# A mixture-of-experts tail: 64-slot chunks started after the first 128-slot chunk, weight places in an explicit queue

## The chip, the core and the metric

One core of a Trainium2 chip runs the whole program in one launch. The metric is device time in microseconds (us) of that core, the median of several executions. Five engines run in parallel: PE (matmul; PEld is its weight load), DVE (vector), ACT (activations), POOL and SP (which here only issues the transfers and reads registers). A profiled execution gives the traces that are quoted below.

## The reference

Two layers of a diffusion backbone over 256 latent and 256 context tokens of width 1024. What matters here is the last stage, the feed-forward part of layer 1: each token goes to the best 2 of 8 experts.

```python
logits = (t @ router_w).astype(float32)              # t: 256 x 1024
top_val, top_idx = lax.top_k(logits, 2)
gate = sum(one_hot(top_idx, 8) * softmax(top_val)[..., None], axis=1)
for e in range(8):
    out += gate[:, e:e+1] * ((silu(t @ w_gate[e]) * (t @ w_up[e])) @ w_down[e])   # 1024 -> 3584 -> 1024
```

All weights are float32 and each is read from HBM once. An expert has 3 x 1024 x 3584 of them.

## The kernel before

An expert's weights are cut into 14 chunks of 256 hidden columns, and a chunk into three units of 128 x 2048 floats (1024 KB): two halves of gate and up (`hf` 0 and 1, four of the eight k-tiles each) and one of down. 8 x 14 x 3 = 336 units are read, one transfer each, all issued by SP in one fixed order.

Two kinds of experts. `full` (lines 1314 to 1362) is for an expert with up to 128 tokens. It splits each half unit into a high and a low part (`split`, lines 232 to 239: ACT writes `wh`, DVE writes `wl`; there are three pairs of buffers) and does three matmuls per product (`mm3`, 245 to 248): 24 of 512 columns for gate and up, 2 transposes, 12 of 512 columns for down. `small` (1379 to 1439) is for an expert with up to 64 tokens and uses the weights as they are, in float32: 16 matmuls of 256 columns (32 passes in the trace) and 4 of 512 (8 passes), two at a time on halves of the array. Expert 0 is a full one. The other seven are put in order by their token count: rank 0 is a full one, ranks 1 to 6 are small ones. So there are 28 full and 84 small chunks. The order is computed on the chip into `ordi` (line 1208), and SP reads it into registers with `values_load` (line 1452) to form the addresses of the weights.

Before the experts, the routing: `L`, the choice `selr`, the slots, then in one block (lines 1176 to 1221) the gate weights (softmax) and the ranking, both chains of small DVE operations. `prep_full` (1250) gathers the tokens of a full expert on PE, `prep_small` (1271) those of three small ones, 8 matmul groups into `es` and three calls of `slots_of`.

Where weights land: `raw_unit` (217 to 230) hands out places in turn: eight `raw` buffers (three in pool `w0`, five in `w3`), and places left over from earlier tiles that `more` lists: `old` (x of the context stream), `old2` and `old3` (parts of the parameter and constant tiles), `spares`. Units 0 to 3 of expert 0 are loaded while attention still runs (line 1092). When `A[:HEAD]` is written out (line 1448), units 4 to 10 go to seven raw buffers. Unit 11, the down part of chunk 3, is asked for later.

The order of the work is the order in which the program calls things, as priorities: a compile-time scheduler fills an engine's idle time with ready work of lower priority. The order is: the four full chunks 0 to 3 of expert 0; the reading of all seven registers; `prep_small`; then 84 steps, one small chunk each, and after every third a full chunk (lines 1456 to 1466), so that the 24 full chunks left are used up at step 71 and the last 12 steps are small alone. A chunk's down part is done with the next chunk (`down(c - 1, ...)`). The last small expert also writes the output.

Of the kernel before, what the change touches and what calls it, by code (L numbers as in the profile page):

```python
# [184 lines left out]
def build(tc, I, out):  # L185
# [26 lines left out]
            n -= w[i]  # L212

    more = []
    newest = []

    def raw_unit(src, n=2048):
        turns["unit"] += 1
        i = turns["unit"] % (len(more) + sum(w[2] for w in wps))
        if i < len(more):  # L220
            r = more[i]()
            if isinstance(r, list):
                for k, h in enumerate(r):
                    nc.sync.dma_start(h, src[:, k * 1024:k * 1024 + 1024])
                return r
        else:
            wp, bufs = ring("raw")
            r = wp.tile([128, n], F32, tag="raw", bufs=bufs, name="raw")
        newest[:] = [nc.sync.dma_start(r, src).ins]
        return r  # L230
# [944 lines left out]
    ordi = sm.tile([128, NR], I32, tag="ordi", bufs=1, name="ordi")  # L1175
    with tc.issue_after(last_mask):

        mxl = sm.tile([128, 2, 4], F32, tag="mxl", bufs=1, name="mxl")
        V.tensor_reduce(out=mxl[:, :, 0], in_=L, axis=AX.X, op=ALU.max)
        V.tensor_tensor(out=L, in0=L, in1=mxl[:, :, 0:1].to_broadcast([128, 2, 8]), op=ALU.subtract)  # L1180
        S.activation(gate, L, AF.Exp)
        V.tensor_tensor(out=gate, in0=gate, in1=selr, op=ALU.mult)
        V.tensor_reduce(out=mxl[:, :, 1], in_=gate, axis=AX.X, op=ALU.add)
        V.reciprocal(mxl[:, :, 2], mxl[:, :, 1])
        V.tensor_tensor(out=gate, in0=gate, in1=mxl[:, :, 2:3].to_broadcast([128, 2, 8]), op=ALU.mult)

        cnt = sm.tile([128, 8], F32, tag="cnt", bufs=1, name="cnt")
        pp = PS()
        for t in range(2):
            PE.matmul(pp[:, 0:8], ones.to_broadcast([128, 128]), selr[:, t], start=t == 0, stop=t == 1)  # L1190
        V.tensor_copy(cnt, pp[:, 0:8])
        r3 = [128, NR, NR]
        ca = cnt[:, None, 1:8].to_broadcast(r3)
        cb = cnt[:, 1:8, None].to_broadcast(r3)
        rg = t1("rg", tuple(r3))
        re_ = t1("rq", tuple(r3))
        V.tensor_tensor(out=rg, in0=ca, in1=cb, op=ALU.is_gt)
        V.tensor_tensor(out=re_, in0=ca, in1=cb, op=ALU.is_equal)
        V.tensor_tensor(out=re_, in0=re_, in1=lt8[:, 1:8, 1:8], op=ALU.mult)
        V.tensor_tensor(out=rg, in0=rg, in1=re_, op=ALU.add)  # L1200
        rk = sm.tile([128, NR], F32, tag="rk", bufs=1, name="rk")
        V.tensor_reduce(out=rk, in_=rg, axis=AX.X, op=ALU.add)
        pm = t1("pm", tuple(r3))
        V.tensor_tensor(out=pm, in0=rk[:, None, :].to_broadcast(r3), in1=C("iota", 0, NR)[:, :, None].to_broadcast(r3),
                        op=ALU.is_equal)
        V.tensor_tensor(out=rg, in0=pm, in1=C("iota", 1, 8)[:, None, :].to_broadcast(r3), op=ALU.mult)
        V.tensor_reduce(out=rk, in_=rg, axis=AX.X, op=ALU.add)
        V.tensor_copy(ordi, rk)

        r4 = [128, 4, NR, NR]  # L1210
        pg = t1("pg", tuple(r4))
        V.tensor_tensor(out=pg, in0=rt.rearrange("p t (a e) -> p (t a) e", a=2)[:, :, None, 1:8].to_broadcast(r4),
                        in1=pm[:, None].to_broadcast(r4), op=ALU.mult)
        V.tensor_reduce(out=slr, in_=pg, axis=AX.X, op=ALU.add)

        V.memset(cap[:, 0:1], 128.0)
        V.tensor_scalar(cap[:, 1:8], pm[:, 0], 64.0, 64.0, op0=ALU.mult, op1=ALU.add)
        V.tensor_tensor(out=cnt, in0=cnt, in1=cap, op=ALU.subtract)
        cmx = sm.tile([128, 2], F32, tag="cmx", bufs=1, name="cmx")
        V.tensor_reduce(out=cmx[:, 0:1], in_=cnt, axis=AX.X, op=ALU.max)  # L1220
        V.tensor_scalar(cnti[:, 0:1], cmx[:, 0:1], 512.0, None, op0=ALU.add)
# [92 lines left out]
    def full(st, e):  # L1314

        yd = []

        def down(c, g):
            if not yd:
                yd.extend(pq.tile([128, 512], F32, tag=f"yd{i}", name=f"yd{i}") for i in range(2))  # L1320
            pt = pq.tile([128, 512], F32, tag="tr", bufs=2, name="tr")
            for m in range(2):
                PE.transpose(pt[:, m * 128:m * 128 + 128], g[:, m * 128:m * 128 + 128], ident)
            hhl = t2("hhl", (128, 2, 256), F32R)
            hh, hl = hhl[:, 0], hhl[:, 1]
            hilo(hh, hl, pt[:, :256])
            for m, wd in enumerate(split_unit(e, c * 3 + 2)):
                for q in range(2):
                    a = slice(q * 512, q * 512 + 512)
                    h = slice(m * 128, m * 128 + 128)  # L1330
                    mm3(yd[q], hh[:, h], hl[:, h], wd[0][:, a], wd[1][:, a], c == 0 and m == 0, c == NCH - 1 and m == 1)

        prev = []

        def chunk(c):
            eh, el = st.e
            if c == 1:
                st.slots()
            ps = pq.tile([128, 512], F32, tag="gu", bufs=2, name="gu")
            for hf in range(2):  # L1340
                for k2, w in enumerate(split_unit(e, c * 3 + hf)):
                    for k in range(2):
                        kt = 4 * hf + 2 * k2 + k
                        a = slice(k * 512, k * 512 + 512)
                        mm3(ps, eh[:, kt], el[:, kt], w[0][:, a], w[1][:, a], kt == 0, kt == 7)
            g = t1("sg")
            S.activation(g, ps[:, :256], AF.Silu)
            V.tensor_tensor(out=g, in0=g, in1=ps[:, 256:], op=ALU.mult)
            if c:
                down(c - 1, prev.pop())  # L1350
            prev.append(g)
            if c == NCH - 1:
                down(c, prev.pop())
                st.y = t8("y", F32R, (128, 2, 1024))
                for q in range(2):
                    a = slice(q * 512, q * 512 + 512)
                    S.activation(st.y[:, 0, a], yd[q], AF.Copy, scale=st.g)
                    V.scalar_tensor_tensor(st.y[:, 1, a], yd[q], st.g, st.y[:, 0, a].bitcast(F32), op0=ALU.mult,
                                           op1=ALU.subtract)
                scatter_full(st)  # L1360

        return [lambda c=c: chunk(c) for c in range(NCH)]

    def add_to(d, ps):
        x = xs[0][:, d]
# [13 lines left out]
    def small(st, e, last=False):  # L1379
# [20 lines left out]
        def chunk(c):  # L1400
            ps = pq.tile([128, 512], F32, tag="gu", bufs=2, name="gu")
            for hf in range(2):
                r = raw_unit(unit_at(e, c * 3 + hf))
                rs = r if isinstance(r, list) else [r[:, 0:1024], r[:, 1024:2048]]
                for k in range(4):
# [5 lines left out]
            g = t1("sg")  # L1411
            S.activation(g[64:], ps[:64, :256], AF.Silu)  # L1412
            V.tensor_tensor(out=g[64:], in0=g[64:], in1=ps[64:, :256], op=ALU.mult)  # L1413
            if c:
                down(c - 1, prev.pop())
            prev.append(g)
            if c == NCH - 1:
# [5 lines left out]
        def scatter_small(st, y):  # L1423
            gT = st.gT.bitcast(F32)
            for d2 in range(2):
                pss = [PS(), PS()]
                for j in range(2):
                    for q in range(2):
                        d = 2 * d2 + j
# [10 lines left out]

    with tc.high_priority(1):
        st0 = prep_full(None, [gate[:, t, 0:1] for t in range(2)], gm0)
    more[:] = [old] + [lambda r=r: r for r in spares[:NPRE]] + [old2, old3]
    turns["unit"] = len(more) - 1
    turns["split"], turns["raw"] = 0, 3
    A = full(st0, 0)
    HEAD = 4
    for f in A[:HEAD]:
        f()
    more[:] = [old, lambda: spares[0], old2, old3]  # L1450
    with tc.issue_after(newest[0]):
        order = [nc.values_load(ordi[0:1, r:r + 1], engines=(mybir.EngineType.SP,), min_val=1, max_val=7)
                 for r in range(NR)]
    small_sts = prep_small([1, 2, 3])
    A = A[HEAD:]
    for i in range(6 * NCH):
        if i == 2 * NCH:
            st1 = prep_full([slr[:, 2 * t + 1, 0:1] for t in range(2)], [slr[:, 2 * t, 0:1] for t in range(2)])
            A += full(st1, order[0])
        if i == 2 * NCH + 8:  # L1460
            small_sts += prep_small([4, 5, 6])
        if i % NCH == 0:
            B = small(small_sts[i // NCH], order[i // NCH + 1], i // NCH == 5)
        B[i % NCH]()
        if i % 3 == 2 and A:
            A.pop(0)()
    over = nc.values_load(cnti[0:1, 0:1], min_val=0, max_val=1024)

    with tc.If(over > 512):
# [9 lines left out]
        with tc.For_i(0, NE, 1) as ei:  # L1479
            re = sm.tile([128, 8], F32, tag="re", bufs=2, name="re")  # L1480
            nc.sync.dma_start(re, rd[bass.ds(ei, 1)].rearrange("a p c -> p (a c)"))
            for n in range(2):
                st = prep_full([re[:, 4 * n + t:4 * n + t + 1] for t in range(2)],
                               [re[:, 4 * n + 2 + t:4 * n + 3 + t] for t in range(2)])
                for f in full(st, ei):
                    f()
        nc.sync.dma_start(out, xs[0])
    dr_close()
    pq_close()
# [22 lines left out]
```

## Time and profile before

| | us |
|---|---|
| median of 3 runs | 1692.71 (1689.86 to 1693.47) |
| profiled execution | 1693.54 |
| its span, first to last instruction | 1691.8 |
| PE matmul busy / weight load busy | 1621.5 (96%) / 1248.8 (74%) |
| DVE / ACT busy | 868.2 (51%) / 642.9 (38%) |
| moved by DMA | 525.25 MB, 310 GB/s over the span |

The busy shares are means over very different stages: read the span in slices first, and then ask in each stage what the engine that matters was waiting for. A "x16" behind a row counts instructions; a time in brackets is the idle time before them and what ended it. SPq is SP's queue: a row there is the moment at which a transfer was issued, not when it landed.

### The profile page before, as it was taken

To read this page: it belongs to the slowest core of one execution; us is meant where nothing else is said; L and a number is where in the kernel's file an instruction comes from. 1 tells how busy PE (TensorE), PEld (TensorE's weight loads), DVE (VectorE), ACT (ScalarE), POOL (GpSimd) and SP (SyncE) were. 2 spreads that over 40 slices of the span, in tenths; PEclk is the share of its full clock that TensorE was granted. 3 is DMA by queue.
4 is the path that set the end of the run, shared out by engine and by line. 5 is a ranking of instruction groups with operands and counts; after the bars stand their busy time and mean duration, and the time that the engine had idled before them with its cause. 6 is when DMAs were issued, how large, how long until landed. Compare 5 with 4: busy or idle time off the path is not lost.

```text
span 1691.8 us, 28517 instructions
## 1 busy us (share of the span) xinstructions
PE 1621.5 (96%) x11576; PEld 1248.8 (74%) x11576; DVE 868.2 (51%) x1484; ACT 642.9 (38%) x1019; POOL 29.2 (2%) x31
## 2 busy tenths in 40 slices
PE   7999999999999999989999999999999999989986
PEld 5897899999999999989876555556565555555643
DVE  4545786688776666667563243335243425233511
ACT  3534574444454444445562232323232323232300
POOL 0100000000000000000100000000000000000000
PEclk9999999999999999999999999999999999999999
DMA  9425266777754666653489999999999999999996
GB/s 375 174 100 200 100 236 222 263 289 298 269 180 167 217 226 252 239 209 129 176 320 400 418 418 419 419 418 419 418 419 419 418 419 418 419 419 419 419 418 261
DMA packets 77901, 525.25 MB, mean 310 GB/s; under 512 B 9024, under 2 KB 9152, under 8 KB 18240
## 3 DMA queue, kind: packets, MB, share of 16 engines
q1 hardware_dynamic: 77760, 523.33, 78.0%
q8 instruction: 93, 1.52, 0.4%
q14 instruction: 48, 0.39, 0.1%
HBM read 522.25 MB, written 1.05 MB: 309 GB/s over the span
## 4 chain that ended last, share of the span: by engine, by line
PE 70%; DMA 23%; DVE 3%; ACT 2%; issue 1%; SPq 0%; POOL 0%; DVEq 0%; ACTq 0%; POOLq 0%
DMA raw<-in_moe 13%; PE gu L1409 10%; PE gu L247 9%; PE gu L248 8%; PE gu L246 8%; DMA prb<-in_moe 6%; PE ys L1395 4%; PE acc L246 4%; PE acc L247 4%; PE acc L248 4%; DMA spare<-in_moe 2%; PE w L247 2%; PE w L248 2%; PE w L246 2%; DMA x<-in_moe 1%; DVE wl L238 1%
## 5 line engine op out<-in xcount | busy, mean ns | idle before, releaser
L238 DVE TENSOR_TENSOR wl<-raw,wh 128x1024 fp32r<-128x1024 f32 x368 | 446.9, 1224 | 216.8 <-ACT wh L236 212.8
L236 ACT ACTIVATE wh<-raw 128x1024 fp32r<-128x1024 f32 x368 | 385.2, 1057 | 331.7 <-PE gu L247 145.5
L248 PE MATMUL gu<-fh,wl 128*128 128x256 f32 x896 | 251.7, 281 | 0.5 <-DVE wl L238 0.5
L246 PE MATMUL gu<-fh,wh 128*128 128x256 f32 x896 | 251.7, 281 | 0.0
L247 PE MATMUL gu<-fl,wh 128*128 128x256 f32 x896 | 250.5, 280 | 0.0
L1409 PE MATMUL gu<-raw,es 128*64 128x256 f32 x1488 | 181.5, 383 | 6.4 <-DMA raw<-in_moe 6.2
L1412 ACT ACTIVATE sg<-gu 64x256 f32<-64x256 f32 x84 | 31.6, 376 | 394.1 <-PE gu L1409 388.6
L246 PEld LDWEIGHTS gu<-fh,wh 128*128 128x128 f32 x896 | 169.0, 189 | 2.7 <-issue 2.7
L247 PEld LDWEIGHTS gu<-fl,wh 128*128 128x128 f32 x896 | 168.4, 188 | 1.0 <-issue 1.0
L248 PEld LDWEIGHTS gu<-fh,wl 128*128 128x128 f32 x896 | 167.8, 187 | 0.7 <-DVE wl L238 0.7
L1413 DVE TENSOR_TENSOR sg<-sg,gu 64x256 f32<-64x256 f32 x84 | 35.6, 424 | 256.4 <-ACT sg L1412 255.9
L1409 PEld LDWEIGHTS gu<-raw,es 128*64 128x64 f32 x1488 | 105.8, 137 | 65.6 <-issue 12.8
L247 PE MATMUL acc<-hl,wh 128*128 128x256 f32 x448 | 124.4, 283 | 0.0
L246 PE MATMUL acc<-hh,wh 128*128 128x256 f32 x448 | 123.8, 282 | 0.0
L248 PE MATMUL acc<-hh,wl 128*128 128x256 f32 x448 | 120.3, 283 | 0.0
L1395 PE MATMUL ys<-raw,hs 128*64 128x512 f32 x424 | 102.3, 597 | 6.6 <-DMA raw<-in_moe 5.4
L247 PE MATMUL gu<-wl,ef 128*128 128x512 f32 x224 | 93.9, 419 | 8.6 <-DVE wl L238 8.5
L246 PE MATMUL gu<-wh,ef 128*128 128x512 f32 x224 | 92.8, 415 | 8.5 <-ACT wh L236 8.5
L248 PE MATMUL gu<-wh,ef 128*128 128x512 f32 x224 | 90.0, 402 | 0.0
L247 PEld LDWEIGHTS acc<-hl,wh 128*128 128x128 f32 x448 | 85.6, 191 | 0.0
L246 PEld LDWEIGHTS acc<-hh,wh 128*128 128x128 f32 x448 | 85.5, 191 | 0.0
L248 PEld LDWEIGHTS acc<-hh,wl 128*128 128x128 f32 x448 | 83.2, 191 | 0.0
(447 smaller groups left out, 2531.3 us busy)
## 6 DMA issues: line engine op xcount, KB each, us to landing
raw<-in_moe SPq DMA_DIRECT2D x223, 1024.0 KB, 17.4
raw<-in_ffn SPq DMA_DIRECT2D x84, 1024.0 KB, 4.9
spare<-in_moe SPq DMA_DIRECT2D x31, 1024.0 KB, 19.6
x<-in_moe SPq DMA_DIRECT2D x28, 1024.0 KB, 19.7
prb<-in_moe SPq DMA_DIRECT2D x27, 1024.0 KB, 18.8
rx<-in_ada SPq DMA_DIRECT2D x19, 1024.0 KB, 5.1
raw<-in_ada SPq DMA_DIRECT2D x18, 1024.0 KB, 4.8
cst<-in_moe SPq DMA_DIRECT2D x27, 512.0 KB, 18.6
```

The costliest lines, as they stand in the source:

```text
L236: S.activation(hi, r, AF.Copy)
L238: V.tensor_tensor(out=lo, in0=r, in1=hi.bitcast(F32), op=ALU.subtract)
L246: PE.matmul(o, wh, rh, start=start, stop=False, **kw)
L247: PE.matmul(o, wh, rl, start=False, stop=False, **kw)
L248: PE.matmul(o, wl, rh, start=False, stop=stop, **kw)
L1395: PE.matmul(yd[0][64 * q:64 * q + 64, :], h[:, m * 64:m * 64 + 64], rs[m][:, q * 512:q * 512 + 512], start=c == 0 and m == 0, stop=c == NC ...
L1409: PE.matmul(ps[64 * q:64 * q + 64, :256], st.e[:, kt], rs[k // 2][:, a:a + 256], start=kt == 0, stop=kt == 7, tile_position=(0, 64 * q))
L1412: S.activation(g[64:], ps[:64, :256], AF.Silu)
L1413: V.tensor_tensor(out=g[64:], in0=g[64:], in1=ps[64:, :256], op=ALU.mult)
```

## The change

After the preloading of expert 0's chunks 0 to 3, now with unit 11 too, only chunk 0 is computed first. Small chunks start right behind it, and the preloaded chunks 1 to 3 are put at steps 5, 11 and 17; the other 24 full chunks are spread over steps 18 to 81. The gate and up part of a full chunk stands ahead of that step's small chunk and its down part behind it. Places come from a queue `places` that starts with four (`spares[0]`, `old2`, `old3`, `old`) and gets two or three raw buffers more as each preloaded chunk has used them. A register is read when its expert's first unit is asked for. The softmax moves behind the ranking. In the last small chunk the down part of the chunk before stands between the two halves, and the last scatter takes its four PSUM banks from two tags of two.

```diff
     def raw_unit(src, n=2048):
-        turns["unit"] += 1
-        i = turns["unit"] % (len(more) + sum(w[2] for w in wps))
+        if places:
+            f = places.pop(0)
+            places.append(f)
+            i = 0 if f else len(more)
+        else:
+            ...
@@ routing: the seven lines of the softmax stand behind V.tensor_copy(ordi, rk) now
@@ full
-            if c:
-                down(c - 1, prev.pop())
             prev.append(g)
+
+        def rest(c):
+            down(c, prev.pop(0))
             if c == NCH - 1:
-                down(c, prev.pop())
                 st.y = t8("y", F32R, (128, 2, 1024))
@@ small
             for hf in range(2):
+                if hf and last and c == NCH - 1:
+                    down(c - 1, prev.pop())
                 r = raw_unit(unit_at(e, c * 3 + hf))
...
-            if c:
+            if prev:
                 down(c - 1, prev.pop())
@@ scatter_small
-                pss = [PS(), PS()]
+                pss = [PS(), PS()] if not last else [
+                    pq.tile([128, 512], F32, tag=t, bufs=2, name="b") for t in ("gu", "tr")]
@@ main order
-    A = full(st0, 0)
-    HEAD = 4
-    for f in A[:HEAD]:
-        f()
-    more[:] = [old, lambda: spares[0], old2, old3]
-    with tc.issue_after(newest[0]):
-        order = [nc.values_load(ordi[0:1, r:r + 1], ...) for r in range(NR)]
+    more[:] = [lambda: spares[0], old2, old3, old]
+    places[:] = [None]
+    for u in range(4, 3 * HEAD):
+        first[u] = raw_unit(unit_at(0, u))
+    places[:] = more
+    def by_rank(r):
+        if r not in order:
+            order[r] = nc.values_load(ordi[0:1, r:r + 1], ...)
+        return order[r]
+    with tc.issue_after(newest[0]):
+        by_rank(1)
+    A = full(st0, 0)
+    A[0][0]()
     small_sts = prep_small([1, 2, 3])
-    A = A[HEAD:]
+    A[0][1]()
+    due = {6 * k - 1: k for k in range(1, HEAD)}
+    i0 = 6 * (HEAD - 1)
+    for k in range(HEAD, 2 * NCH):
+        due[i0 + (k - HEAD) * (6 * NCH - i0) // (2 * NCH - HEAD)] = k
     for i in range(6 * NCH):
...
+        k = due.get(i)
+        if k is not None:
+            A[k][0]()
         B[i % NCH]()
-        if i % 3 == 2 and A:
-            A.pop(0)()
+        if k is not None:
+            A[k][1]()
+            if k < HEAD:
+                places += [None] * (2 if k == 1 else 3)
```

## Rows read from the trace of the kernel before

**Rows 1.** The page: the span in 40 slices of 42.3 us.
```profile
DMA  9425266777754666653489999999999999999996
GB/s 375 174 100 200 100 236 222 263 289 298 269 180 167 217 226 252 239 209 129 176 320 400 418 418 419 419 418 419 418 419 419 418 419 418 419 419 419 419 418 261
```

**Rows 2.** Windows: length, busy PE, PEld, DVE, ACT, POOL, clock, DMA share, GB/s.
```profile
843.58:930.00 86.42, 86.42 (x486) 59.76 (x486) 45.63 (x57) 42.59 (x61) 0.00 (x0) 1.00 0.91 353
846.00:858.00 12.00, 12.00 (x58) 10.06 (x58) 10.08 (x12) 10.30 (x15) 0.00 (x0) 1.00 1.00 396
930.00:1660.00 730.00, 695.01 (x4254) 408.53 (x4250) 261.03 (x414) 196.07 (x285) 0.00 (x0) 0.99 1.01 419
```

**Rows 3.** Timeline of SP: when transfers of expert weights were issued (start, length).
```profile
823.12 1.42 SPq L229 DMA_DIRECT2D raw<-in_moe  x2
843.58 0.36 SPq L229 DMA_DIRECT2D spare<-in_moe  x1
...
845.92 0.33 SPq L229 DMA_DIRECT2D raw<-in_moe  x1
```

**Rows 4.** Lines 1208, 1452: count, ns min/median/max, first and last start.
```profile
L1208 DVE CAST ordi<-rk x1: 161/161/161, 838.9 to 838.9; 128x7 int32<-128x7 f32 x1
L1452 SPq TENSOR_LOAD <-ordi x7: 262/263/472, 839.1 to 842.8; - x7
```

**Rows 5.** Landing times of tile `spare` (815 to 1000) and of `raw` (800 to 845).
```profile
DMA to landing us min/median/max: 4.7/10.1/18.9
...
DMA to landing us min/median/max: 4.8/6.6/9.6
```

**Rows 6.** Timeline of the head, and its group for line 1280 (busy, mean ns).
```profile
842.26 0.48 PE L246 MATMUL gu<-wh,ef 128*128 128x512 f32 x1
847.86 1.28 ACT L1347 ACT_TABLE_LOAD   x1
854.91 1.23 DVE L238 TENSOR_TENSOR wl<-x,wh 128x1024 fp32r<-128x1024 f32 x1 [0.44 <-ACT wh L236]
L1280 PE MATMUL b<-gms,ht 128*128 128x192 f32 x32 | 6.7, 326 | 0.0
862.55 0.51 PE L1241 MATMUL b<-slr,gms 128*128 128x1 f32 x4
```

**Rows 7.** The chain that ended last, 905 to 925: start, length, what.
```profile
909.50 0.23 PE yd L246
...
912.05 0.26 PE tr L1388 x2
912.32 3.38 PE gu L1409 x29
...
917.69 0.27 PE tr L1388 x2
```

**Rows 8.** Timeline after the last full chunk: PE, until it waits for a transfer again.
```profile
1599.90 0.73 PE L1374 MATMUL b<-gT,y 128*128 128x256 f32 x4
1623.79 1.95 PE L1409 MATMUL gu<-raw,es 128*64 128x256 f32 x16 [0.55 <-DMA raw<-in_moe]
```

**Rows 9.** Timeline of the end.
```profile
1672.43 1.95 PE L1409 MATMUL gu<-raw,es 128*64 128x256 f32 x16 [0.45 <-DMA raw<-in_moe]
1674.42 0.38 ACT L1412 ACTIVATE sg<-gu 64x256 f32<-64x256 f32 x1 [7.09 <-PE gu L1409]
1674.83 0.42 DVE L1413 TENSOR_TENSOR sg<-sg,gu 64x256 f32<-64x256 f32 x1 [4.76 <-ACT sg L1412]
1675.02 1.94 PE L1395 MATMUL ys<-x,hs 128*64 128x512 f32 x8 [0.64 <-DMA x<-in_moe]
1677.26 0.29 DVE L1390 COPY hs<-tr 128x128 f32<-128x128 f32 x1 [2.00 <-PE tr L1388]
1677.60 1.94 PE L1395 MATMUL ys<-spare,hs 128*64 128x512 f32 x8 [0.38 <-DVE hs L1390]
1683.20 1.13 PE L1430 MATMUL b<-gT,ys 64*128 64x256 f32 x4 [0.89 <-DVE x L1366]
```

More of the change, by code (lines that the diff above doesn't have):

```diff
@@ L214, in build @@
     more = []
+    places = []
     newest = []
     def raw_unit(src, n=2048):
-        turns["unit"] += 1
-        i = turns["unit"] % (len(more) + sum(w[2] for w in wps))
+        if places:
[3 more added lines that the diff above has]
+        else:
+            turns["unit"] += 1
+            i = turns["unit"] % (len(more) + sum(w[2] for w in wps))
+            f = more[i] if i < len(more) else None
         if i < len(more):
-            r = more[i]()
+            r = f()
             if isinstance(r, list):
                 for k, h in enumerate(r):
-                    nc.sync.dma_start(h, src[:, k * 1024:k * 1024 + 1024])
+                    newest[:] = [nc.sync.dma_start(h, src[:, k * 1024:k * 1024 + 1024]).ins]
                 return r
@@ L1176, in build @@
     with tc.issue_after(last_mask):
[L1178 to L1185, printed above, removed]
         cnt = sm.tile([128, 8], F32, tag="cnt", bufs=1, name="cnt")
@@ L1208, in build @@
         V.tensor_copy(ordi, rk)
+        mxl = sm.tile([128, 2, 4], F32, tag="mxl", bufs=1, name="mxl")
+        V.tensor_reduce(out=mxl[:, :, 0], in_=L, axis=AX.X, op=ALU.max)
+        V.tensor_tensor(out=L, in0=L, in1=mxl[:, :, 0:1].to_broadcast([128, 2, 8]), op=ALU.subtract)
+        S.activation(gate, L, AF.Exp)
+        V.tensor_tensor(out=gate, in0=gate, in1=selr, op=ALU.mult)
+        V.tensor_reduce(out=mxl[:, :, 1], in_=gate, axis=AX.X, op=ALU.add)
+        V.reciprocal(mxl[:, :, 2], mxl[:, :, 1])
+        V.tensor_tensor(out=gate, in0=gate, in1=mxl[:, :, 2:3].to_broadcast([128, 2, 8]), op=ALU.mult)
         r4 = [128, 4, NR, NR]
@@ L1360, in chunk @@
                 scatter_full(st)
-        return [lambda c=c: chunk(c) for c in range(NCH)]
+        return [(lambda c=c: chunk(c), lambda c=c: rest(c)) for c in range(NCH)]
     def add_to(d, ps):
@@ L1442, in build @@
         st0 = prep_full(None, [gate[:, t, 0:1] for t in range(2)], gm0)
-    more[:] = [old] + [lambda r=r: r for r in spares[:NPRE]] + [old2, old3]
-    turns["unit"] = len(more) - 1
+    HEAD = 4
     turns["split"], turns["raw"] = 0, 3
-    A = full(st0, 0)
-    HEAD = 4
-    for f in A[:HEAD]:
-        f()
-    more[:] = [old, lambda: spares[0], old2, old3]
-    with tc.issue_after(newest[0]):
-        order = [nc.values_load(ordi[0:1, r:r + 1], engines=(mybir.EngineType.SP,), min_val=1, max_val=7)
-                 for r in range(NR)]
-    small_sts = prep_small([1, 2, 3])
-    A = A[HEAD:]
+    more[:] = [lambda: spares[0], old2, old3, old]
[3 more added lines that the diff above has]
+    places[:] = more
+    order = {}
+    def by_rank(r):
+        if r not in order:
+            order[r] = nc.values_load(ordi[0:1, r:r + 1], engines=(mybir.EngineType.SP,), min_val=1, max_val=7)
+        return order[r]
+    with tc.issue_after(newest[0]):
+        by_rank(1)
+    A = full(st0, 0)
+    A[0][0]()
+    small_sts = prep_small([1, 2, 3])
+    A[0][1]()
[3 more added lines that the diff above has]
+        due[i0 + (k - HEAD) * (6 * NCH - i0) // (2 * NCH - HEAD)] = k
     for i in range(6 * NCH):
@@ L1458, in build @@
             st1 = prep_full([slr[:, 2 * t + 1, 0:1] for t in range(2)], [slr[:, 2 * t, 0:1] for t in range(2)])
-            A += full(st1, order[0])
+            A += full(st1, by_rank(0))
         if i == 2 * NCH + 8:
@@ L1462, in build @@
         if i % NCH == 0:
-            B = small(small_sts[i // NCH], order[i // NCH + 1], i // NCH == 5)
+            B = small(small_sts[i // NCH], by_rank(i // NCH + 1), i // NCH == 5)
+        k = due.get(i)
+        if k is not None:
+            A[k][0]()
         B[i % NCH]()
-        if i % 3 == 2 and A:
-            A.pop(0)()
+        if k is not None:
+            A[k][1]()
+            if k < HEAD:
+                places += [None] * (2 if k == 1 else 3)
+    places[:] = []
+    turns["unit"] = 0
     over = nc.values_load(cnti[0:1, 0:1], min_val=0, max_val=1024)
@@ L1484, in build @@
                                [re[:, 4 * n + 2 + t:4 * n + 3 + t] for t in range(2)])
-                for f in full(st, ei):
-                    f()
+                for k, f in enumerate(steps := full(st, ei)):
+                    f[0]()
+                    if k:
+                        steps[k - 1][1]()
+                steps[-1][1]()
         nc.sync.dma_start(out, xs[0])
```

## The prediction

> **What bounds the kernel now.** I read the page's slices first [rows 1]. From slice 23 on the DMA engines are busy in nine tenths or more and move 418 or 419 GB/s, whatever PE does; in slices 19 to 21 they move 129, 176 and 320 GB/s. So the last half of the span is set by the reading of weights, and the stretch before it wastes reading time. The windows say the same [rows 2]: 930 to 1660 runs at 419 GB/s and a DMA share of 1.01, 843.58 (the first transfer of a routed expert) to 930 at 353. A unit of 1.049 MB therefore takes 2.50 us of reading, and a small or full chunk 7.5 us. SP's timeline [rows 3] shows where the stretch begins: expert 0's seven raw units are issued by 824.5, then nothing for 19 us. The two lines of the order [rows 4] tell why: `ordi` is written from 838.92 to 839.08, seven register reads begin at 839.1, and the first routed transfer is issued at 843.58. Last I read the end [rows 9] for what follows the last landing, and the dense stretches of PE [rows 7] for what a chunk costs it: a small one 5.64 us (transposes at 912.05 to transposes at 917.69), a full one 36 x 0.23 + 0.3 for its transposes, with switches some 8.9 us.
>
> Everything up to 824 is untouched. The end moves by what the stream of transfers gains or loses, plus what comes after its last landing. I work against the profiled execution's own 1693.54 us (span 1691.8); the median of the runs, 1692.71, lies 0.8 lower, and I put the sum on the median.
>
> **The change part by part.**
>
> *Register read when needed, ranking before softmax.* Seven reads and their address arithmetic took 839.1 to 843.5, 0.63 us each [rows 3, 4]. One is left ahead of the first transfer: 6 x 0.63 = 3.8 us earlier. The two DVE chains alternate now; the ranking first should save the two delays of 0.2 us or so that it suffers, 0.4 us. The softmax finishes that much later, behind the gathering for expert 0, which keeps PE until 842. First routed transfer at 839.4: **-4.2 us** (bounds -3.7 to -4.5). The six other reads are met later in SP's queue; there SP issues one transfer in 2.5 us of reading and waits for a place in between, so 0.6 us each costs nothing, and 0.6 each where that cover is missing.
>
> *Unit 11 preloaded.* The eighth raw buffer was first used at 845.92 [rows 3], though no expert weight is read from about 830 to 843. It is now filled with unit 11 behind the seventh, in idle reading time, so one unit less has to be read afterwards: **-2.5 us** (bounds -2.5 to 0, should the buffer come free late).
>
> *What the reading loses after its first routed transfer.* Before: (419 - 353)/419 x 86.4 = 13.6 us up to 930 [rows 2], partly its start, mostly waiting for raw buffers that four full chunks hold. After: the start costs 4.7 us to the first landing [rows 5] less 2.5 of reading, 2.2. Only four places exist at first, and the fourth, `old`, holds the down weights of chunk 0, so four units are in by about 854 and then the reading stops until PE has done half a small chunk. PE starts at 842.26 and must first do chunk 0's gate and up (to 847.9, where ACT loads silu's table), `prep_small` (32 instructions, 8 x 0.65 = 5.2; three `slots_of` at some 0.6 = 1.9), and chunk 0's down part, 0.3 + 12 x 0.23 = 3.1 [rows 6, 7]: 858.1. The first half unit takes 1.7 more (half of 3.38). If the scheduler fills gaps as it did before, where pieces of `prep_small` stood between matmuls, I take 858.3 for the fifth transfer's issue (bounds 854.5 and 861). It lands at 863.0, where unbroken reading would have had it at 844.1 + 4 x 2.5 = 854.1: 8.9 lost.
>
> From there four places must sustain the rate. A place's round is 4.7 to land, 1.95 of matmuls, about 0.4 to release and issue: 7.1 us, against the 10.0 us that four units take to read. It holds with 2.9 us to spare. A shallow queue read 396 GB/s in 846 to 858 [rows 2], 5.5% under the deep one: over some 26 us, 1.5 us. Chunk 1's gate and up at step 5 keep PE for 5.6 us, 2.7 more than the spare time, if they stand in one piece; filled into PE's gaps of 7.5 - 5.64 = 1.9 us per small chunk they cost nothing; I take 1.0. After that six, nine and twelve places carry any full chunk. Sum 2.2 + 8.9 + 1.5 + 1.0 = 13.6 us, the same as before: **0 us** (bounds -7 and +8). What was a wait for raw buffers becomes a wait for the first small chunk.
>
> *Spreading the full chunks.* 2.75 small chunks per full one ask 2.75 x 5.64 + 8.9 = 24.4 us of PE in 28.1 us of reading, so the reading still sets the pace: **0**. It ends with the last full chunk at step 81 instead of 71. When it and its scatter were done before, at 1600.6, PE was behind: it ran 22.6 us without a wait, to 1623.2, through 12 units that take 30.0 us to read [rows 8]. It was 7.4 us late, 2.8 of it because two down parts stood together, now one: 4.6. A small unit gives back (7.5 - 5.64)/3 = 0.62 us. After step 81 six units are left, three of which may be done ahead of the scatter: 0.9 to 2.7 us late at the end. **+1.8 us** (bounds 0 and +5).
>
> *The last chunk.* Before, the last but one landing released the down part (1675.02) and the last one came in time for 1677.60 [rows 9]. Now the second half lands last but one, at about 1675.0 on that scale, and 1.95 + 0.38 + 0.42 + transposes 0.27 + copy 0.29 with their gaps, 3.6 us, follow before the last down part: 1678.5 against 1677.6, **+0.9** (bounds 0 and +1.6). Two more PSUM tags remove the 0.89 us that the last scatter matmuls waited; the eight additions, at 0.41 one after the other, then end 0.4 us earlier: **-0.4** (bounds -0.9 and 0).
>
> **Sum:** -4.2 - 2.5 + 0 + 0 + 1.8 + 0.9 - 0.4 = -4.4 us. 1692.7 - 4.4 = **1688.3 us**.
>
> The Trainium skill speaks against the four places: in DMA: Bandwidth & Descriptors, section Bandwidth, 1 MB moved by itself reaches 341 GB/s, 16 MB 425. The row with a shallow queue shows 396 here, so the trace agrees in direction. By the page's figure 26 us of reading would lose 4.8 us and not 1.5, and the estimate would be 1691.6.
>
> **The rivals.**
>
> *1. Gain and new loss cancel.* The first small chunk starts only at 861 (+2.7), chunk 1 stands in one piece (+1.7): 1692.7. For it: every routed transfer past the fourth waits for PE, and PE has no gap from 842 to 858. Against it: `prep_small` was mixed finely with other work. The case that PE, not the reading, sets the pace belongs here: PE is busy 695 of 730 us in 930 to 1660 [rows 2], and no PE work is removed, so the time would stay within a microsecond. The rate of 419 GB/s without a dip, and weight loads busy only 409 of these 730, speak against it.
>
> *2. Four places starve the reading (slower).* If a place's round in the first six steps is not 7.1 but over 10 us, each microsecond costs 18/4 = 4.5 us over their 18 units. The preloads took up to 9.6 us to land [rows 5]; 9.6 + 1.95 + 0.4 = 12.0 gives +9.0, and the time is 1697.3. It turns the forecast to a loss from a round of about 11 us. Against it: a 9.6 us landing needs other transfers in front, which four places hardly allow.
>
> *3. The head overlaps better.* Small matmuls fill PE's gaps from 848 on, the fifth transfer goes out at 854.5 and chunk 1 costs nothing: -3.8 - 1.0, with no lag at the end -1.8: 1681.7. For it: the scheduler did put other work between full matmuls [rows 6]. Against it: nothing shows PE idle in this stretch.
>
> **How the numbers follow.** The measurement tells about 0.2%, 3.4 us, from no change. Forecast 0.42 (nearly all of it faster: 0.38), rival 1 0.33, rival 2 0.13, rival 3 0.12. Faster 0.38 + 0.12 = 0.50; same 0.04 + 0.33 = 0.37; slower 0.13. The range reaches from rival 3 to the middle of the way to rival 2, 1682.0 to 1694.5; the forecast case alone is 1685 to 1691.
>
> **What would show it.** In the changed trace: SP issues the first routed transfer near 839.4, with one register read ahead; an eighth raw unit is issued before 830; the fifth routed transfer near 858.3; the mean rate from the first routed transfer to 930 again near 353 GB/s. After 930 it stays at 419. Near the end PE does not wait for the last units, or waits less than before. I am wrong on the sum if the reading is even from 845 on (rival 3), if rates under 380 GB/s go on past step 6 (rival 2), or if the time from the last landing to the end grows by over 5 us.

## The result and the profile after

The changed kernel takes 1714.18 us (median of 4 runs, 1711.92 to 1715.52) against 1693.09 for the kernel before beside it: ratio 1.0121, 95% interval 1.0102 to 1.014. It is slower by 21 us; I had forecast 1688.3 and a range up to 1694.5. The profiled execution took 1714.5, its span is 1712.7, so the two spans differ by 20.9 us.

The page's slices of the changed kernel, against [rows 1]:

```profile
DMA  9425366777644666652689599999999999999995
GB/s 377 165 99 197 121 223 219 287 290 285 262 176 164 218 250 245 240 212 108 246 329 400 227 416 419 418 419 418 419 418 419 419 419 419 418 419 419 419 419 228
```

Slices 19 to 22 (108, 246, 329, 400) are much as before. New is a hole where 418 had stood: slice 23 (942 to 985) moves 227 GB/s. The windows place it (columns as in [rows 2]):

```profile
838.54:930.00 91.46, 82.91 (x530) 50.96 (x529) 25.78 (x48) 25.46 (x45) 0.00 (x0) 0.98 0.86 332
930.00:980.00 50.00, 37.91 (x226) 20.51 (x224) 11.61 (x18) 8.89 (x13) 0.00 (x0) 0.92 0.64 255
980.00:1680.00 700.00, 676.22 (x3988) 383.76 (x3989) 264.70 (x401) 203.04 (x292) 0.00 (x0) 1.00 1.01 419
```

From 930 to 980 the reading loses (419 - 255)/419 x 50 = 19.6 us; after that it is as even as before. SP's timeline shows both ends of the head and of the hole (start, length; it answers to [rows 3]):

```profile
799.90 22.38 SPq L236 DMA_DIRECT2D raw<-in_moe  x8
838.54 0.36 SPq L236 DMA_DIRECT2D spare<-in_moe  x1
...
848.79 0.34 SPq L236 DMA_DIRECT2D x<-in_moe  x1
855.92 0.33 SPq L236 DMA_DIRECT2D spare<-in_moe  x1
...
867.76 0.33 SPq L236 DMA_DIRECT2D spare<-in_moe  x1
...
930.16 0.33 SPq L236 DMA_DIRECT2D spare<-in_moe  x1
930.70 25.59 SPq L236 DMA_DIRECT2D raw<-in_moe  x2
956.56 0.33 SPq L236 DMA_DIRECT2D prb<-in_moe  x1
957.14 0.33 SPq L231 DMA_DIRECT2D cst<-in_moe  x1
```

Two transfers into `raw` stand in one row of 25.59 us: the first goes out at 930.70, the second at 955.96, and everything behind it in SP's fixed order (`prb`, `cst`, `x`, `spare`) waits with it. SP's waits from 905 to 965 (total, times, longest) name the one that held it:

```profile
SPq L236 <- DVE wl L245: 24.7, 1, 24.7
```

And the timeline before and around its end:

```profile
915.61 2.96 PE L1418 MATMUL gu<-raw,es 128*64 128x256 f32 x16
...
940.41 1.23 DVE L245 TENSOR_TENSOR wl<-raw,wh 128x1024 fp32r<-128x1024 f32 x1 [6.99 <-ACT wh L243]
...
945.61 1.22 DVE L245 TENSOR_TENSOR wl<-raw,wh 128x1024 fp32r<-128x1024 f32 x1 [0.73 <-ACT wh L243]
...
951.86 0.50 PE L253 MATMUL yd<-wh,hhl 128*128 128x512 f32 x1
...
954.51 0.39 PE L255 MATMUL yd<-wh,hhl 128*128 128x512 f32 x1
954.71 2.54 DVE L245 TENSOR_TENSOR wl<-raw,wh 128x1024 fp32r<-128x1024 f32 x2 [1.90 <-ACT wh L243]
...
955.96 0.33 SPq L236 DMA_DIRECT2D raw<-in_moe  x1
...
960.76 1.98 PE L1402 MATMUL ys<-raw,hs 128*64 128x512 f32 x4 [5.60 <-DMA raw<-in_moe]
```

The transfer waits for a split (`wl`) that empties its buffer: it goes out at 955.96, and the first of the two splits in the row of 954.71 ends at 955.93. Counted through from chunk 0, this is the second half of unit 9. Unit 9 belongs to chunk 3 of expert 0, the third preloaded one, whose turn is step 17; its split needs a `wh` and a `wl` buffer that chunk 2's down part (`yd`, to 954.9) has just given back. So the buffer that SP wanted from 931 on was not one that a finished chunk had freed: it was one still full.

In the code an entry `None` of `places` says only "a raw buffer"; which pool it comes from is told by `ring("raw")`, whose eight turns, counted from unit 4 on, are five of pool `w3` and then three of `w0`. Units 4 to 8 had taken the five turns of `w3`, units 9 to 11 the three of `w0`. The queue's first five raw transfers (906.18, 906.72, 916.45, 918.61, 930.70) fell to `w3` again and had to wait there for 1.6 us at most. They did not go into five different buffers: the last splits of units 7 and 8, counted in the same way, are the rows of 940.41 and 945.61, and the transfer of 918.61 waited for the matmuls in the row of 915.61, a small chunk that read what the transfer of 906.18 had brought. SP's waits from 916.9 to 919:

```profile
SPq L236 <- PE gu L1418: 1.6, 1, 1.6
```

The sixth raw transfer is the turn of `w0`. All three buffers there held units of chunk 3, and it had to wait for the first of them, while in `w3` the buffer of the transfer of 916.45, read until 932.5, lay free. PE ran dry at 955.2 and stood for 5.60 us (the last row of the timeline), until that transfer had landed.

At the end (against [rows 9]):

```profile
1692.58 1.89 PE L1402 MATMUL ys<-raw,hs 128*64 128x512 f32 x8
1694.30 1.90 PE L1418 MATMUL gu<-raw,es 128*64 128x256 f32 x16
1697.13 0.33 PE L1395 MATMUL tr<-cst,sg 64*128 64x64 f32 x2 [0.94 <-DVE sg L1422]
1697.85 1.94 PE L1402 MATMUL ys<-raw,hs 128*64 128x512 f32 x8 [0.38 <-DVE hs L1397]
1700.57 2.00 PE L1440 MATMUL b<-gT,ys 64*128 64x256 f32 x16 [0.79 <-ACT ys L1429]
1701.74 3.22 DVE L1373 SCALAR_TENSOR_TENSOR x<-b,ada,x 128x256 f32<-128x256 f32 x8 [3.95 <-PE b L1440]
```

The last unit lands at 1693.75 by the landing records (1677.35 before): 16.4 of the 20.9 us. PE doesn't wait for it, nor for the one before, as it did in [rows 9]: it is late. From the last landing to the end of the last addition it is 1704.96 - 1693.75 = 11.2 us, before 7.9. The remaining 1.2 us lie behind that addition, where 5.6 to 7.8 us passed in all these kernels with the same work: a difference between executions that nothing here explains.

### The profile page after: what moved, and what is told of

Its sections match the earlier page's. It is cut to its first block, busy times and chain, and to the rows that moved or that the text cites. A ratio compares the mean times of both kernels' runs of the same rounds, so it can differ in the third digit from the quotient of the medians.

```text
span 1712.7 us, 28498 instructions
## 1 busy us (share of the span) xinstructions
PE 1635.3 (95%) x11576; PEld 1235.7 (72%) x11576; DVE 865.8 (51%) x1484; ACT 641.0 (37%) x1019; POOL 29.2 (2%) x31
## 5 line engine op out<-in xcount | busy, mean ns | idle before, releaser
L245 DVE TENSOR_TENSOR wl<-raw,wh 128x1024 fp32r<-128x1024 f32 x332 | 402.3, 1223 | 214.8 <-ACT wh L243 213.1
L243 ACT ACTIVATE wh<-raw 128x1024 fp32r<-128x1024 f32 x332 | 346.9, 1057 | 323.3 <-PE gu L254 146.5
L1418 PE MATMUL gu<-raw,es 128*64 128x256 f32 x1424 | 175.5, 386 | 0.9 <-DMA raw<-in_moe 0.9
L1418 PEld LDWEIGHTS gu<-raw,es 128*64 128x64 f32 x1424 | 96.5, 137 | 69.2 <-issue 26.1
L1402 PE MATMUL ys<-raw,hs 128*64 128x512 f32 x440 | 109.3, 620 | 12.3 <-DMA raw<-in_moe 11.2
```

What stands on the lines that cost most here:

```text
L243: S.activation(hi, r, AF.Copy)
L245: V.tensor_tensor(out=lo, in0=r, in1=hi.bitcast(F32), op=ALU.subtract)
L1402: PE.matmul(yd[0][64 * q:64 * q + 64, :], h[:, m * 64:m * 64 + 64], rs[m][:, q * 512:q * 512 + 512], start=c == 0 and m == 0, stop=c == NC ...
L1418: PE.matmul(ps[64 * q:64 * q + 64, :256], st.e[:, kt], rs[k // 2][:, a:a + 256], start=kt == 0, stop=kt == 7, tile_position=(0, 64 * q))
```

## The experiments

Medians with the ratio to the kernel before in the same session (1692.1 us for experiments 1 to 4, 1694.35 for 5 to 8, 1693.45 for 9 to 12). "1, ..." in the second column means the kernel of experiment 1 with that further edit.

| | kernel | us | ratio (95%) |
|---|---|---|---|
| 1 | freed raw buffers named as places | 1704.35 | 1.0076 (1.0063 to 1.0089) |
| 2 | ring kept, raw places only after chunk 3 (four runs: two at 1699 to 1700, two at 1709) | 1704.37 | 1.0068 (1.0043 to 1.0092) |
| 3 | 1, last full chunk at step 71 | 1696.43 | 1.0032 (1.002 to 1.0044) |
| 4 | before, with late registers and ranking first | 1691.61 | 1.0004 (0.9989 to 1.0019) |
| 5 | 1, second full expert lighter | 1700.39 | 1.0039 (1.0021 to 1.0058) |
| 6 | 3, three chunks preloaded | 1686.59 | 0.9966 (0.9951 to 0.998) |
| 7 | 3, old end | 1695.11 | one run |
| 8 | 4, unit 11 preloaded | 1693.13 | 0.9995 (0.9983 to 1.0008) |
| 9 | 1, full chunk behind the small one | 1693.63 | 1.001 (1.0001 to 1.002) |
| 10 | 1, expert 0 lighter | 1695.29 | 1.0015 (1.0004 to 1.0027) |
| 11 | 6, old end | 1686.65 | 0.9964 (0.9952 to 0.9976) |
| 12 | 6, spread to step 81 | 1696.43 | 1.002 (1.0007 to 1.0033) |

### Is it the ring's turn? (1 and 2)

Experiment 1 changes nothing but which raw buffer a new place is:

```diff
-                places += [None] * (2 if k == 1 else 3)
+                places += [lambda r=first[u]: r for u in range(max(4, 3 * k), 3 * k + 3)]
```

> The queue's raw places name the very buffers that a preloaded chunk has just freed, instead of taking the next of the ring of eight. Theory (the ring): the changed kernel stood from 930.7 to 956.3 because the ring's turn had come to the buffer of unit 9, which chunk 3 still held, though the buffers of units 4 and 5 had long been used up and free. Then SP's wait of 24.7 us on wl is gone, the 19.6 us of reading lost between 940 and 980 come back, and the time is 1694 to 1696 us. Rival (too few places: any six places would have been empty while PE does chunk 2 at step 11): at most a third comes back, 1707 us or more. What is lost at 850 to 870 and 890 to 920 (about 15 us) stays under both.

Experiment 2 keeps the ring and adds its eight buffers only when chunk 3 is done:

```diff
-            if k < HEAD:
-                places += [None] * (2 if k == 1 else 3)
+            if k == HEAD - 1:
+                places += [None] * 8
```

> The ring is kept, but all eight raw places are added at once after chunk 3 (step 17), when none is held any more; steps 0 to 17 run on four places. Theory (the ring): no wait of SP over 10 us in the head; each of chunks 1 to 3 costs at most 5 us of reading, so 1695 to 1705 us, faster than the changed kernel with fewer places for longer. Rival (too few places): four places for twelve more steps lose more, 1716 us or above.

The windows of experiment 1:

```profile
930.00:980.00 50.00, 47.03 (x305) 25.98 (x302) 14.06 (x24) 9.69 (x15) 0.00 (x0) 1.00 1.01 418
1200.00:1250.00 50.00, 43.33 (x238) 25.27 (x237) 15.50 (x21) 12.69 (x17) 0.00 (x0) 0.93 1.01 419
1250.00:1310.00 60.00, 55.72 (x339) 32.71 (x337) 27.21 (x45) 17.79 (x25) 0.00 (x0) 1.00 0.87 344
```

The hole is gone, 418 where 255 stood, and so is the wait of 24.7 us; experiment 2 has no long wait for `wl` either (6.2 us in all from 830 to 1060). (It loses 12.0 us more evenly, 377 GB/s from 930 to 1050, since its places come late.) That the ring's turn made the first hole is shown. But the time fell by only 10 us, not by 19.6: a second hole opened, (419 - 344)/419 x 60 = 10.7 us from 1250 to 1310, where the changed kernel ran at 419. Experiment 2, set back by its 12.0 us, runs at 419 there too.

### What is the second hole? (5, 9, 10)

Counting landed and consumed units in the trace, PE falls from 1 unit behind the reading at 1100 to 10 behind at 1300; with the part that is in work all twelve places are then held, and SP waits for PE and for splits. In the changed kernel the first hole had set the reading back, and by the same count PE was under six units behind there. PE is idle for 6.7 of the 50 us before the hole, though units lie ready. Its timeline there:

```profile
1203.09 1.90 PE L1418 MATMUL gu<-raw,es 128*64 128x256 f32 x16
1205.92 0.33 PE L1395 MATMUL tr<-cst,sg 64*128 64x64 f32 x2 [0.94 <-DVE sg L1422]
1206.54 0.50 PE L253 MATMUL gu<-wh,ef 128*128 128x512 f32 x1 [0.29 <-ACT wh L243]
1207.80 0.55 PE L254 MATMUL gu<-wl,ef 128*128 128x512 f32 x1 [0.76 <-DVE wl L245]
1208.15 0.63 PE L255 MATMUL gu<-wh,ef 128*128 128x512 f32 x1
...
1212.02 0.39 PE L253 MATMUL gu<-wh,ef 128*128 128x512 f32 x1
```

At this passage from a small to a full chunk PE meets a row of waits, since its order is fixed at compile time: transposes that need the small chunk's `sg`, then `wh`, then `wl`. Waits of 0.94, 0.29 and 0.77 come back one full chunk later, from 1239.73 on. Experiment 5 made the wrong chunks lighter:

```diff
-                        mm3(ps, eh[:, kt], el[:, kt], w[0][:, a], w[1][:, a], kt == 0, kt == 7)
+                        (mm3 if isinstance(e, int) else mm2)(ps, eh[:, kt], el[:, kt], w[0][:, a], w[1][:, a],
+                                                             kt == 0, kt == 7)
```

(the down product likewise; `mm2` is `mm3` without its second matmul of `wh`.)

> The kernel with each freed raw buffer named as a place (the first experiment), in which the second full expert (rank 0, 14 chunks) is left without the product of the high part of the weights and the low part of the tokens: two matmuls per product instead of three, 12 fewer per chunk, 12 x 0.23 = 2.8 us less of PE work in each of its chunks and some 39 us over the expert. That part of the computation is left out. Theory (the reading loss of about 10.7 us between 1250 and 1310 comes from PE, which consumes a unit in about 2.9 us there while the reading delivers one in 2.50, until all twelve places are held): the rates of 1250 to 1310 stay above 400 GB/s, no wait of SP for PE over 5 us in 1200 to 1400, and the time falls by about 10 us against the first experiment, to 1692 to 1697. Rival (the places or the order of the queue still hold the reading up there, whatever PE has to do): the rates of 1250 to 1310 fall to 250 to 390 again and the time stays within 3 us of 1704.

The dip stayed (344 from 1250 to 1310), and this says nothing on PE: expert 0's fourteen chunks run up to 1300, so the lightened expert begins behind the stretch. (What it gained is behind the dip: from the last landing to the end of the last addition 9.3 us, in experiment 1 11.1.) Experiment 10 puts the same edit where it bears (`mm2 if isinstance(e, int) and c > 3`):

> As the experiment that lightened the second full expert, but for expert 0, whose chunks are the ones that run up to 1300: its chunks 4 to 13 are left without the product of the high part of the weights and the low part of the tokens, 12 matmuls x 0.23 = 2.8 us less of PE work in each; that part of the computation is left out. Seven of these chunks fall into 1100 to 1300: 19 us less work where PE fell 9 units of 2.5 us behind the reading. Theory (PE's pace there fills all twelve places and stops the reading): PE's arrears stay under six units, the rates of 1250 to 1310 stay above 400 GB/s and the time is 1693 to 1697. Rival (something else than PE's pace holds the places): the loss of 10 us stays, 1702 to 1706.

```profile
1200.00:1250.00 50.00, 40.23 (x246) 20.65 (x242) 15.40 (x23) 13.30 (x19) 0.00 (x0) 1.00 1.01 419
1250.00:1310.00 60.00, 56.24 (x345) 33.03 (x345) 29.46 (x49) 19.05 (x27) 0.00 (x0) 1.00 1.01 418
```

No dip, and 1695.29: PE's pace holds the places there. (By the count above PE was at most 3.4 units behind from 1100 to 1310, inside what I expected.) Experiment 9 leaves all work in and moves a full chunk behind its step's small one, as before:

```diff
-        if k is not None:
+        if k is not None and k < HEAD:
             A[k][0]()
         B[i % NCH]()
+        if k is not None and k >= HEAD:
+            A[k][0]()
         if k is not None:
             A[k][1]()
```

> The kernel with each freed raw buffer named as a place (the first experiment, 1704.3), with both parts of a full chunk behind the small chunk of its step, as before; the three preloaded chunks stay as they are. In the first experiment PE is idle for 6.7 of the 50 us from 1200 to 1250, in waits for the splits of a full chunk that stand behind the activation of the small one, though 7 to 10 units lie there unused. Theory (the order around a full chunk makes these waits): PE busy over 47 of 50 us in 1200 to 1250, no rate under 400 GB/s in 1250 to 1310, about 1694. Rival (the waits come from when the units land, or from the amount of work, and not from this order): the loss of some 10 us stays and the time is 1702 to 1706.

```profile
1200.00:1250.00 50.00, 48.28 (x294) 28.92 (x295) 20.40 (x30) 16.09 (x22) 0.00 (x0) 1.00 1.02 419
1250.00:1310.00 60.00, 58.26 (x356) 34.55 (x354) 27.58 (x45) 18.15 (x25) 0.00 (x0) 1.00 1.01 416
```

The whole work is the same, and in 1200 to 1250 PE is busy for 48.28 us instead of 43.33, there is no dip, and the time is 10.7 us less than in experiment 1. Absolute windows catch the two executions at slightly different work (the first routed transfer went out at 842.27 in experiment 1 and at 835.51 here), so I take a longer one as well, experiment 1 first:

```profile
1100.00:1300.00 200.00, 185.65 (x1102) 110.66 (x1100) 75.30 (x128) 57.19 (x89) 0.00 (x0) 0.98 0.99 405
```

```profile
1100.00:1300.00 200.00, 195.09 (x1176) 117.54 (x1175) 84.22 (x138) 64.96 (x97) 0.00 (x0) 1.00 1.01 418
```

PE is idle for 14.4 us in one and 4.9 in the other. So with the same work the order around a full chunk decides whether the second hole opens. It is not the only way to close it: less work closes it too (experiment 10). The edit also puts the full chunk's transfers behind the small one's in SP's queue; which of the two orders matters was not separated.

The Trainium skill (Perfetto Trace Analysis, section Optimization Strategy) says that the same gap repeating on the engine that should be saturated can mean too few buffers for the next tile. Here most of the gaps went with the same buffers in another order (PE's waits in 1200 to 1250 fall from 6.6 us to 1.7), so in this case the measurement decides against that reading.

### The spread, the head and the end (3, 6, 12, 7, 11)

Experiment 3 ends the full chunks at step 71, as before:

```diff
-        due[i0 + (k - HEAD) * (6 * NCH - i0) // (2 * NCH - HEAD)] = k
+        due[i0 + (k - HEAD) * (5 * NCH + 4 - i0) // (2 * NCH - HEAD)] = k
```

> As e1_own, and the last full chunk stands at step 71 instead of 81 (the spacing is 2.33 small chunks). Theory of the tail: PE is late at the end because only six units follow the last full chunk; with 36 it catches up, and the time from the last landing to the end falls from about 18.6 us to about 15, so 3 to 4 us less than e1_own. Rival: the last landing itself moves later by as much because full chunks stand denser, and the time is that of e1_own within 1 us.

It gains 7.9 us: from the last landing to the end of the last addition 11.1 us become 8.3 (2.8), and the second hole shrinks (385 GB/s from 1250 to 1310, 4.9 us instead of 10.7). Experiment 6 then preloads three chunks, so that three raw buffers are places from the start:

```diff
-    HEAD = 4
+    HEAD = 3
-    places[:] = more
+    held = []
+    for _ in range(3):
+        wp, bufs = ring("raw")
+        held.append(wp.tile([128, 2048], F32, tag="raw", bufs=bufs, name="raw"))
+    places[:] = more[:3] + [lambda r=r: r for r in held] + more[3:]
```

> The kernel with own places and with the last full chunk at step 71 (the third experiment, 1696.4), with three of expert 0's chunks preloaded instead of four, so that three raw buffers are places from the start: seven places, not four. Theory (four places starve the reading in the head): SP's idle time between the fourth and the eighth routed transfer, some 11 us, shrinks to about 3, and the dips of 890 to 910 go, 11 us in all, but three units or 7.5 us more are left to read: about 1692 to 1693. Rival (the head is held by PE, which has chunk 0, the gathering and the first chunks to do whatever the places are, so the gain only moves the wait to the next place that PE must free): the three units cost their 7.5 us and the time is 1700 to 1704.

```profile
836.66:930.00 93.34, 92.16 (x610) 58.08 (x609) 29.43 (x52) 29.02 (x51) 0.00 (x0) 1.00 0.95 385
...
1200.00:1250.00 50.00, 49.81 (x301) 29.31 (x301) 23.57 (x39) 18.54 (x29) 0.00 (x0) 1.00 1.01 417
1250.00:1310.00 60.00, 57.95 (x342) 33.62 (x342) 23.64 (x36) 16.25 (x22) 0.00 (x0) 1.00 1.01 419
```

1686.59: faster than both kernels, against before by 0.34% (0.2 to 0.49). From its first routed transfer (836.66) to 930 the reading loses (419 - 385)/419 x 93.34 = 7.6 us; in the changed kernel, from 838.54 on, 19.0. That is 11.4 won for 7.5 paid, much as expected. I had expected 1692.5 in all; the rest is the second hole, 4.9 us in experiment 3, which isn't there. Experiment 12 asks why not, by spreading its full chunks to step 81 again:

> The kernel with three preloaded chunks, with the other 25 full chunks spread over steps 12 to 81 instead of 12 to 71, as in the change. Theory (three preloaded chunks remove the head's loss and keep PE under the limit of the places; the late full chunks cost only at the end): no rate under 400 GB/s between 930 and 1660, from the last landing to the end 3 to 4 us more than 14.0, the time about 1690. Rival (the shorter spread is what keeps PE on pace in 1200 to 1310): the dip comes back, 1698 or more.

```profile
1250.00:1310.00 60.00, 58.42 (x350) 33.15 (x350) 23.13 (x43) 14.60 (x23) 0.00 (x0) 0.97 0.99 388
```

The dip is back, as the rival had it (its time of 1698 is not reached), and with the longer end (11.3 us from the last landing to the end of the last addition, 8.3 in experiment 6) it costs 10 us. The amount of work done doesn't explain it: by 1100 experiment 6 has done 9.7 full chunks and is 1.8 units behind, this one 8.4 and 4.8. Which property of the spread makes the scheduler's order leave fewer waits is open.

Experiments 7 and 11 put the down part of the last chunk but one back behind both halves:

```diff
-                if hf and last and c == NCH - 1:
-                    down(c - 1, prev.pop())
```

> The kernel with own places and the last full chunk at step 71, with the down part of the last chunk but one behind the last gate and up again, as before. Theory (the down part between the halves costs what I predicted, 0.9 us, since the second half is then late): from the last landing to the end 13.0 us instead of 13.9. Rival (the end hangs on work behind the last matmul alone): 13.9, no difference over 0.3.

> The kernel with three preloaded chunks (1686.6), with the down part of the last chunk but one behind the last gate and up again. From the earlier look at that edit, which shortened the stretch from the last landing to the end from 13.9 to 12.85: 1.0 us less, about 1685.6. Rival (that look showed a scatter of one execution): 1686.6, no difference.

From the last landing to the end of the last addition: 8.28 us to 7.25 in the first pair, 8.28 to 7.35 in the second. (The first pair has one run of the kernel with the old end.) The stretch is shorter by what the prediction put on it; in the time of the whole, 1686.65 against 1686.59, a microsecond is not seen.

### The two gains alone (4 and 8)

Both on the kernel before, with its order and its turn of places: 4 reads a register when it is needed and puts the ranking first (of its edit only the reading is shown here), 8 also preloads unit 11.

```diff
-        order = [nc.values_load(ordi[0:1, r:r + 1], ...) for r in range(NR)]
+        by_rank(1)
```

> The kernel before with two edits of the change alone: a register is read when its expert is due, and the softmax stands behind the ranking. Theory of the prediction's first term: the first routed transfer goes out 4 us earlier and the end moves by 4 us, to 1689 us. Rival: after four early units the reading waits for raw buffers that the full chunks free on PE's time (before: issues at 853.0, 859.6, 863.3), so the 4 us are given back within 15 us and the time stays within 1 us of before.

```diff
+    for u in range(4, 3 * HEAD):
+        first[u] = raw_unit(unit_at(0, u))
+    turns["unit"] = 12
     A = full(st0, 0)
```

> The kernel before with registers read when needed, the ranking ahead of the softmax, and unit 11 preloaded into the eighth raw buffer; order, turn of the buffers and all else as before. Theory of the prediction (a unit read ahead of the routing is one unit less to read afterwards): 2.5 us less than with late registers alone, about 1689. Rival (the reading of 840 to 930 is bound by the places that PE has to free, so an earlier unit only waits in its buffer and holds that place longer): within 1 us of 1691.6.

The same window of both, 4 first:

```profile
843.58:930.00 86.42, 86.42 (x487) 58.91 (x486) 44.11 (x54) 39.86 (x57) 0.00 (x0) 1.00 0.88 342
```

```profile
843.58:930.00 86.42, 86.42 (x487) 58.61 (x487) 43.82 (x54) 39.69 (x57) 0.00 (x0) 1.00 0.84 331
```

The first routed transfer goes out at 836.88 and 836.58, 6.7 and 7.0 us earlier than before (3.3 and 3.6 of it because all work up to there ran earlier in these executions: the first preload at 798.27 and 797.96, before at 801.55), and unit 11 is there. But the mean rate falls from 353 [rows 2] to 342 and 331, and PE is busy for all of the 86.42 us in each. The last unit lands 2.4 and 2.5 us earlier than before, less than that shift alone, and neither time differs from before by 0.2%. Units that come earlier wait earlier for PE to free a place.

## Why the prediction was wrong

What it had right: the start (first routed transfer at 838.54, forecast 839.4; the first register read came at 837.5, 1.6 us earlier than in [rows 4], since the work ahead ran earlier), the eighth raw unit ahead of 830, one register read ahead (the six others were not met later in the queue, as I had thought: they came from 841.6 to 844.4, while SP had to wait for the fifth place anyway), the fifth routed transfer at 855.92 (forecast 858.3, bounds 854.5 to 861), 419 GB/s from 980 to 1680.

The step that failed is the sentence "After that six, nine and twelve places carry any full chunk", which closed the term of what the reading loses. I counted places and did not ask which buffer each entry was. I had described the raw buffers as added when a chunk has used them; the code only adds turns. The diff that I quoted has `None` entries, and `raw_unit` sends them to the ring; laid beside the preloaded units, the sixth turn falls on the pool whose three buffers hold units 9 to 11. With buffers of its own the same queue runs at 418 GB/s from 930 to 980 (experiment 1). This is 19.6 us, outside the bounds of -7 and +8 on that term. None of the three rivals had it.

The same term was 5.4 us too low before 930 as well: 19.0 lost from 838.54 on, not 13.6. The place `spare` came round at 855.92, 867.76, 879.30 and 893.09, in 11.5 to 13.8 us, over the 10.0 that four units take to read. I had put 7.1, with 4.7 for the landing and no wait for PE. The landings of `spare` from 855 to 900:

```profile
DMA to landing us min/median/max: 4.9/6.7/9.4
```

In the three rounds the landing took 4.9, 9.4 and 7.9 us, and in the first and the third the unit then lay for 5.0 and 3.9 us until PE, busy with other work, read it. This is the second rival, whose 9.6 us for a landing I had argued away. Experiment 6, with three places more, loses 7.6 us there and not 19.0.

The term of the spread, "so the reading still sets the pace: 0", looks right in the changed kernel only because its reading had been set back. Without the ring's fault it costs 10.7 us. I had divided PE's work (24.4 us) by the reading time (28.1) and left out two things: the waits inside PE's fixed order, 14.4 us from 1100 to 1300 in experiment 1, and the gathering and scattering of tokens where experts change, some 24 us of busy PE in the same 200 us (gathering 11.4, scattering 8.6, slots 3.7). The time that my division leaves free there, 200 x (28.1 - 24.4)/28.1 = 26 us, does not hold both.

The two gains, -4.2 and -2.5, are real as events and worth nothing as time in the order of before (experiments 4 and 8). My first rival named this (gain and loss cancel, with PE as the pace), at 0.33. What they are worth in the changed order was not run.

The end was about right: +0.9 + 1.8 - 0.4 = +2.3 forecast, 11.2 - 7.9 = 3.3 measured. By parts: the down part between the halves 1.0 and 0.9 (experiments 7 and 11; forecast 0.9), PE's lateness 2.8 (experiment 3; forecast 1.8), the PSUM tags, from the start of the last scatter to the end of the additions, 4.92 to 4.39, -0.5 (forecast -0.4).

The sum against the profiled executions: -5.0 (start) - 2.5 (unit 11) + 5.4 (head) + 19.6 (hole) + 3.3 (end) + 1.2 (behind the last addition) = 22.0, measured 20.9. Of the 1.1 left over, 1.0 lies in the last 17.35 us before the last landing, where the reading lost 4.3 us before (316 GB/s) and loses 3.3 now (340).

So the mended change (own buffers, three preloaded chunks, the last full chunk at step 71 as before) is worth 0.34%. Mended in the buffers alone it is still 12 us slower than the kernel before (experiment 1). Three chunks together with full chunks behind the small ones were not run.

## What to carry to other kernels

When one engine issues all transfers in a fixed order, write out for each issue which buffer it goes into and what must have read it; a count of free places proves nothing, and one place taken too early stops all that are free behind it. A transfer that starts earlier is only worth something if the place after it also comes free earlier. And a hole upstream hides those downstream: mend it, and look at the whole trace again.

## What the runs showed of the hardware

In two places PE's granted clock was low after a wait, and the wait cost more than its length. The windows of the changed kernel after the wait of 5.60 us, and of experiment 1 after three waits of 0.94, 0.29 and 0.76 us within 2.8 us:

```profile
960.80:964.00 3.20, 3.20 (x8) 0.96 (x10) 0.00 (x0) 0.00 (x0) 0.00 (x0) 0.50 0.92 358
```

```profile
1208.20:1211.00 2.80, 2.80 (x8) 2.21 (x7) 1.82 (x2) 1.09 (x2) 0.00 (x0) 0.50 1.02 415
```

The granted clock is 0.50, 1.2 of its levels of 1.2 and 2.4 GHz. The matmuls of 512 columns start 0.43 us apart from 1208.15 on and 0.23 later, so eight of them cost 1.6 us more, nearly as much as the three waits together. At the passage to the down part, from 1222.08 on, with waits of 0.93, 0.29 and 0.54 us, the clock held. What separates the two is not shown here.
